# Encoder block in fp32 on one core: another order of the opening, unread matmuls in TensorE's waits, and tiles on 512-byte addresses

## The chip, the core and the metric

The kernel runs on one core of a Trainium2 chip. The metric is device time in microseconds. Before the change three executions took 1934.24, 1934.75 and 1935.72 us, median 1934.75.

## The reference, cut to what matters

One layer with 256 tokens and width 2048, all in float32:

```
mod = silu(c) @ w_ada + b_ada            # c is one vector of 2048; mod is 9 vectors of 2048
sh1,sc1,gt1, sh2,sc2,gt2, sh3,sc3,gt3 = split(mod, 9)
n   = rms_norm(x, g_ffn1) * (1 + sc1) + sh1
h   = x + 0.5*gt1 * ((silu(n @ w1_gate) * (n @ w1_up)) @ w1_down)     # 2048 -> 5632 -> 2048
n   = rms_norm(h, g_mix) * (1 + sc2) + sh2
q,k,v = split(n @ w_qkv);  o = attention(q, k, v)                     # 16 heads of 128
h   = h + gt2 * (o @ w_o)
n   = rms_norm(h, g_ffn2) * (1 + sc3) + sh3
out = h + 0.5*gt3 * ((silu(n @ w2_gate) * (n @ w2_up)) @ w2_down)
```

## The kernel before

**Layout.** The activations lie transposed, features on the 128 partitions and the 256 tokens along them: `h` is 16 tiles (k = 0 to 15) of 128x256, loaded as four DMAs of 512 KB (`h<-in_x_dram`, L515). Each weight is streamed once as 656 tiles of 128x1024 (`rw`, 512 KB, one DMA of SyncE's queue each, L77), four of them in flight. To keep float32's precision, each weight tile is split: ScalarE writes the rounded part (`hiw`, L84), VectorE the rest (`low`, L91), and a product is three matmuls in the fp32r format (`mm3`, L222 to 225): high by high, high by low, low by high. The activations are split in the same way: `nx[k]` holds both parts of tile k of the normed input, side by side, `hd` of the hidden layer, `ox` of the attention's output.

**Order.** The order on each engine is that in which the code issues; no scheduler moves anything. A class `Flow` counts units, one weight tile each: `step()` (L114) splits the tiles ahead of their use and runs what was due; `before1` (L552) does this by hand for the first units. The work goes: opening; first half-FFN up (`up_start`, L405, for the first K1 = 3 tiles k and two column groups of 1024, into all eight PSUM banks `pa`; then `up_pass`, banks `pu`), down (`ffn_down`, L433, banks `pd`); norm; q, k, v and attention (`pqv`, `pqk`, `pqq`, then `psc`, `po`); output projection (`pso`); norm; second half-FFN.

**Modulation.** `mod` is made on VectorE: for a vector j and a tile k, two instructions of 128x1024 (`ada_use`, L196) multiply a tile of `w_ada` with silu(c), which lies spread over all partitions in `cb`, and sum it into one column of `acc`. The 288 tiles of `w_ada` (512 KB each) go through SyncE's queue too.

**The opening** (L501 to L567): DMAs of c, spread over the partitions by the DMA (2 x 512 KB), of the vectors `vec` (112 KB), of the modulation tiles (1, 0) and (0, 0) (scale and shift of tile 0; 4 x 512 KB), then x, then weights and the modulation tiles of k = 1 and 2. ScalarE and VectorE make silu(c) on `cb`; VectorE sums the four modulation tiles of k = 0; ScalarE squares x (L538), and 16 float32 matmuls with a matrix of ones (L540) sum the squares into `pstat`. Then follow the factor of the norm `rs` (`rstd_act`, L245 and 246, on ScalarE, `rstd_dve`, L250 to 253, on VectorE), tile 0's norm (`p0` L305 on VectorE, `p1` L308 on ScalarE, `p2` L311 on VectorE) and the first two weight tiles' split. For k = 1 and 2 VectorE first sums four modulation tiles, then norms, then splits.

**The two later norms.** `Stat.finish` (L290) sums the squares by two float32 matmuls: L292 for those of all tiles but the last, L293 for the last, which VectorE has just squared (L272). Then the same factor and norm follow, and TensorE has no other work until the first `nx` is there.

Of the kernel before, what the change touches and what calls it, by code (L numbers as in the profile page):

```python
# [15 lines left out]
P = 128  # L16
S = 256
# [133 lines left out]
def build(tc, a):  # L151
    nc = tc.nc
    with ExitStack() as ctx:
# [15 lines left out]
        epst = cp.tile([P, 1], F32, name="epst")  # L169
        nc.vector.memset(epst, EPS)  # L170
# [3 lines left out]
        G1, GO, BA = 0, 48, 80  # L174
# [10 lines left out]
        gat = cp.tile([P, 2, KT], F32, name="gat")  # L185

        def ada_use(j, k, b, raw):
# [6 lines left out]
            if b == 1:  # L194
                init = acc[:, j, 0, k : k + 1]
            nc.vector.tensor_tensor_reduce(  # L196
                out=raw, in0=raw, in1=cb[:, b * CW : (b + 1) * CW], scale=scale, scalar=init,
                op0=ALU.mult, op1=ALU.add, accum_out=acc[:, j, b, k : k + 1])
# [5 lines left out]
        def mod(j, k):  # L204
            assert (j, k) in modded, (j, k)
            return acc[:, j, 1, k : k + 1]
# [33 lines left out]
        def rstd_tiles(w, tag):  # L240
            ts = [sp.tile([P, S], F32, tag="nt", bufs=4, name="rt")[:, :w] for i in range(2)]
            return ts + [sp.tile([P, w], F32, tag=tag, bufs=2, name=tag)]

        def rstd_act(ps, n, ts):
            nc.scalar.activation(ts[0], ps, AF.Ln, scale=1.0 / n, bias=epst)  # L245
# [15 lines left out]
        class Stat:  # L261
# [28 lines left out]
            def finish(self):  # L290
                self.ps = bank("pstat")[:, :S]
                nc.tensor.matmul(self.ps, ones, self.acc, start=True, stop=False)  # L292
                nc.tensor.matmul(self.ps, ones, self.last, start=False, stop=True)  # L293

# [138 lines left out]
        def ffn_down(jg, stat=None, out=None):  # L433
# [54 lines left out]
            if stat is not None:  # L488
                stat.add(stat.square(h[d], True))
                stat.finish()  # L490
# [10 lines left out]
        nc.sync.dma_start(cb[:, :CW], a["c"][0].partition_broadcast(P))  # L501
        nc.sync.dma_start(vec, a["vecs"])
        nc.sync.dma_start(cb[:, CW:], a["c"][1].partition_broadcast(P))
        early = {}

        def early_load(k):
            for j in (1, 0):
                t = big("ra")
                for b in range(2):
                    early[k, j, b] = t[:, 4 * b : 4 * b + 4, :].rearrange("p a s -> p (a s)")  # L510
                    nc.sync.dma_start(early[k, j, b], a["w_ada"][j * KT + k, b])

        early_load(0)
        for q in range(4):
            nc.sync.dma_start(h4[q], a["x"][q])  # L515
        fl.fetch(1)
        for k in range(1, K1):
            early_load(k)
            fl.fetch(min(2 * k + 1, RAWW - 1))
        thc = big("thc")  # L520
        for b in range(2):
            th = thc[:, 4 * b : 4 * b + 4, :].rearrange("p a s -> p (a s)")
            cs = slice(b * CW, (b + 1) * CW)
            nc.scalar.activation(th, cb[:, cs], AF.Tanh, scale=0.5)
            nc.vector.scalar_tensor_tensor(cb[:, cs], th, 1.0, cb[:, cs], ALU.add, ALU.mult)
        ln_exp_set()
        bias3 = vec[:, BA : BA + 9 * KT].rearrange("p (n j k) -> p n j k", n=3, j=3)
# [6 lines left out]
        for q in range(4):  # L534
# [4 lines left out]
            for i in range(4):  # L539
                nc.tensor.matmul(ps1, ones, sq[:, i, :], start=q + i == 0, stop=q + i == 6)  # L540
        rt = rstd_tiles(S, "rs")

        def early_use(k):
            for j in (1, 0):
                for b in range(2):
                    ada_use(j, k, b, early[k, j, b])
# [5 lines left out]
        def before1(k, j):  # L552
            if j == 0:
                early_use(k)
                if k == 0:
                    rstd_act(ps1, D, rt)
                    rstd_dve(ps1, D, rt)
                norm_now(k, rt[2], 1, 0)
# [4 lines left out]
            fl.to_hi(fl.u)  # L563
            fl.to_lo(fl.u)
            fl.u += 1
            return fl.hi.pop(fl.u - 1), fl.lo.pop(fl.u - 1)
# [408 lines left out]
```

## Time and profile before

| | us |
|---|---|
| median of three runs | 1934.75 |
| the profiled execution, its own time | 1935.05 |
| its span, from the first to the last instruction | 1933.2 |
| TensorE busy | 1890.7 (98%) |
| VectorE busy | 1527.3 (79%) |
| ScalarE busy | 895.7 (46%) |
| first matmul | 15.35 |
| first matmul of `up_start` | 29.92 |

Names before and behind the arrow are the tiles written and read; a count stands behind an x. PE is TensorE, DVE VectorE, ACT ScalarE, SP SyncE, SPq its sequencer. Matmuls overlap: how often TensorE takes one is read from the distance between two starts, not from an instruction's own duration. In the table by windows, PEclk is the clock granted to TensorE as a share of full speed.

### The profile page before, as it was taken

What the parts mean: (1) busy time and instruction counts of PE and PEld (TensorE: products, weight loads), DVE (VectorE), ACT (ScalarE), POOL (GpSimd) and SP (SyncE); (2) the same over time, 40 slices, a digit from 0 to 9 for tenths busy, and PEclk for the clock granted to TensorE, in tenths of its full rate; (3) what the DMA queues carried; (4) which work ended last, traced back from release to release, by engine and by line L of the source; (5) the groups of instructions that cost most, each with busy time, mean ns of one, the idle gap of its engine ahead of it and who ended that gap; (6) DMA issues with size and microseconds to landing.
All of it is one profiled execution on the core that took longest, in us unless ns stands there. A gap on an engine that the chain in (4) does not pass through costs nothing.

```text
span 1933.2 us, 24958 instructions
## 1 busy us (share of the span) xinstructions
PE 1890.7 (98%) x9024; PEld 1582.3 (82%) x9024; DVE 1527.3 (79%) x2082; ACT 895.7 (46%) x1223; POOL 0.7 (0%) x6
## 2 busy tenths in 40 slices
PE   5999999999999999999999998999999999999999
PEld 4788888888888888788888997888888888888887
DVE  5889988888898889678887988777787888876444
ACT  3664444444444444455555544654443544443432
POOL 0000000000000000000000000000000000000000
PEclk8999999999999999999999999999999999999999
DMA  8899987777799999576766656998888777787664
GB/s 308 325 350 308 311 294 251 248 247 258 244 348 353 350 368 343 196 241 215 249 202 214 206 182 198 307 308 277 273 270 268 222 211 226 215 289 250 201 195 126
DMA packets 141101, 504.89 MB, mean 261 GB/s; under 512 B 15665, under 2 KB 17969, under 8 KB 140977
## 3 DMA queue, kind: packets, MB, share of 16 engines
q1 hardware_dynamic: 140976, 503.30, 77.9%
q8 instruction: 70, 1.15, 0.2%
q14 instruction: 55, 0.44, 0.1%
HBM read 501.14 MB, written 2.10 MB: 260 GB/s over the span
## 4 chain that ended last, share of the span: by engine, by line
PE 93%; DVE 5%; DMA 1%; ACT 0%; issue 0%; SPq 0%; DVEq 0%; ACTq 0%
PE pu L223 16%; PE pu L225 16%; PE pu L224 16%; PE pd L225 6%; PE pd L223 6%; PE pd L224 6%; PE pd L228 4%; PE pd L229 2%; PE pqv L223 2%; DVE low L91 2%; PE pqv L225 2%; PE pqv L224 2%; PE pqk L223 2%; PE pqk L224 2%; PE pqk L225 2%; PE pqq L223 2%
## 5 line engine op out<-in xcount | busy, mean ns | idle before, releaser
L84 ACT CAST hiw<-rw 128x1024 fp32r<-128x1024 f32 x656 | 692.0, 1056 | 960.8 <-PE pu L225 449.6
L91 DVE TENSOR_TENSOR low<-rw,hiw 128x1024 fp32r<-128x1024 f32 x656 | 802.2, 1224 | 346.3 <-issue 132.1
L223 PE MATMUL pu<-hiw,nx 128*128 128x512 f32 x1352 | 527.9, 390 | 0.4 <-ACT pt L348 0.4
L225 PE MATMUL pu<-hiw,nx 128*128 128x512 f32 x1352 | 526.3, 389 | 0.0
L224 PE MATMUL pu<-low,nx 128*128 128x512 f32 x1352 | 526.1, 389 | 0.0
L223 PEld LDWEIGHTS pu<-hiw,nx 128*128 128x128 f32 x1352 | 253.8, 188 | 52.9 <-ACT pt L348 0.8
L225 PEld LDWEIGHTS pu<-hiw,nx 128*128 128x128 f32 x1352 | 253.7, 188 | 52.9
L224 PEld LDWEIGHTS pu<-low,nx 128*128 128x128 f32 x1352 | 253.8, 188 | 52.2
L223 PE MATMUL pd<-hiw,hd 128*128 128x512 f32 x528 | 207.5, 393 | 0.0
L225 PE MATMUL pd<-hiw,hd 128*128 128x512 f32 x528 | 207.3, 393 | 0.0
L224 PE MATMUL pd<-low,hd 128*128 128x512 f32 x528 | 205.6, 389 | 0.0
L196 DVE CUSTOM_DVE_ANT_0 ra<-ra,cb,acc 128x1024 f32<-128x1024 f32 x144 | 187.2, 1300 | 0.2
L228 PE MATMUL pd<-hd,hiw 128*128 128x512 f32 x352 | 124.7, 398 | 0.0
L224 PEld LDWEIGHTS pd<-low,hd 128*128 128x128 f32 x528 | 99.1, 188 | 22.2
L225 PEld LDWEIGHTS pd<-hiw,hd 128*128 128x128 f32 x528 | 99.2, 188 | 22.1
L223 PEld LDWEIGHTS pd<-hiw,hd 128*128 128x128 f32 x528 | 99.2, 188 | 20.4
L352 DVE TENSOR_TENSOR pt<-pt,pu 128x512 f32<-128x512 f32 x176 | 112.5, 680 | 0.0
L229 PE MATMUL pd<-hd,low 128*128 128x256 f32 x352 | 98.9, 281 | 0.0
L196 DVE CUSTOM_DVE_ANT_0 ra<-ra,cb,vec 128x1024 f32<-128x1024 f32 x64 | 81.9, 1279 | 0.0
L228 PEld LDWEIGHTS pd<-hd,hiw 128*128 128x128 f32 x352 | 66.2, 188 | 16.2
L223 PE MATMUL pso<-ox,hiw 128*128 128x256 f32 x256 | 73.1, 285 | 0.0
L225 PE MATMUL pso<-ox,low 128*128 128x256 f32 x256 | 72.4, 283 | 0.0
(139 smaller groups left out, 1972.6 us busy)
## 6 DMA issues: line engine op xcount, KB each, us to landing
ra<-in_w_ada_dram SPq DMA_DIRECT2D x288, 512.0 KB, 5.0
rw<-in_w_d_dram SPq DMA_DIRECT2D x176, 512.0 KB, 4.6
rw<-in_w_c_dram SPq DMA_DIRECT2D x154, 512.0 KB, 4.3
rw<-in_w_b_dram SPq DMA_DIRECT2D x121, 512.0 KB, 4.8
rw<-in_w_qkv_dram SPq DMA_DIRECT2D x96, 512.0 KB, 3.8
rw<-in_w_a_dram SPq DMA_DIRECT2D x63, 512.0 KB, 4.9
rw<-in_w_o_dram SPq DMA_DIRECT2D x32, 512.0 KB, 3.8
rw<-in_w_s_dram SPq DMA_DIRECT2D x14, 512.0 KB, 4.3
```

Of the source, the lines that this page charges most:

```text
L84: self.nc.scalar.copy(t, self.raw[self.nhi])
L91: self.nc.vector.tensor_tensor(t, self.raw.pop(self.nlo), self.hi[self.nlo].bitcast(F32), ALU.subtract)
L196: nc.vector.tensor_tensor_reduce(out=raw, in0=raw, in1=cb[:, b * CW : (b + 1) * CW], scale=scale, scalar=init, op0=ALU.mult, op1=ALU.add, ...
L223: nc.tensor.matmul(out, lh, rh, start=first, stop=False, **kw)
L224: nc.tensor.matmul(out, lh, rl, start=False, stop=False, **kw)
L225: nc.tensor.matmul(out, ll, rh, start=False, stop=last, **kw)
L228: nc.tensor.matmul(ps, lh, r.rearrange("p t s -> p (t s)"), start=first, stop=False)
L229: nc.tensor.matmul(ps[:, :S], ll, r[:, 0, :], start=False, stop=last)
L352: nc.vector.tensor_tensor(part[G][:, j, t, :], part[G][:, j, t, :], ps[t], ALU.add)
```

## The change

**DMA order.** x is loaded right behind `vec`, then the scale's modulation tiles of k = 0, then `w_zero` (2 x 512 KB: the columns of `w_ada` that make the shift of tile 0, with the contraction on the partitions), then the first weight tiles. c is no longer loaded spread. On SyncE's queue the opening was (`cb` is c, `ra` a modulation tile, `h` is x, `rw` a weight tile):

```order
L501 DMA cb<-in_c_dram 128x1024
L502 DMA vec<-in_vecs_dram 128x224
L503 DMA cb<-in_c_dram 128x1024
L511 DMA ra<-in_w_ada_dram 128x1024 x4
L515 DMA h_80<-in_x_dram 128x1024
L515 DMA h_81<-in_x_dram 128x1024
L515 DMA h_82<-in_x_dram 128x1024
L515 DMA h_83<-in_x_dram 128x1024
L77 DMA rw<-in_w_s_dram 128x1024 x2
```

and in the changed kernel it is:

```order
L515 DMA vec<-in_vecs_dram 128x224
L517 DMA h_78<-in_x_dram 128x1024
L517 DMA h_79<-in_x_dram 128x1024
L517 DMA h_80<-in_x_dram 128x1024
L517 DMA h_81<-in_x_dram 128x1024
L521 DMA ra<-in_w_ada_dram 128x1024 x2
L523 DMA wz<-in_w_zero_dram 128x1024 x2
L77 DMA rw<-in_w_s_dram 128x1024 x2
```

Six DMAs of 512 KB no longer stand ahead of x.

**c on 16 columns.** silu(c) is made on a 128x16 tile (`sc2`, printed `sc`). VectorE multiplies the identity with its columns (`dg`, four of 128x512), four float32 matmuls with the ones spread them over the partitions into PSUM (`pc`), and ScalarE copies them into `cb` between the squares of x.

**Squares and shift.** VectorE adds the squares in pairs, so that 8 float32 matmuls of 256 columns are left of 16. The shift of tile 0 comes of 16 float32 matmuls of one column each (`pm`) and one small VectorE instruction (`shift0`).

**Unread matmuls.** Fp32r matmuls of 512 columns go into a bank `idle` that nobody reads: 7 at the start, 4 behind each quarter of the squares, and at the two later norms 4 between the two sums and 13 behind them. TensorE's order in the opening was (`pstat` the sums of squares, `pa` the first product):

```order
L540 MATMUL pstat<-sq_151,ones 128x256 x8
L540 MATMUL pstat<-sq_162,ones 128x256 x8
L223 MATMUL pa_176<-hiw,nx_85 128x512
L224 MATMUL pa_176<-low,nx_85 128x512
L225 MATMUL pa_176<-hiw,nx_85 128x512
```

and is:

```order
L536 MATMUL idle<-nx_97 128x512 x7
L551 MATMUL pc<-dg,ones 128x512 x4
L569 MATMUL pstat<-sq_172,ones 128x256 x2
L536 MATMUL idle<-nx_97 128x512 x4
L569 MATMUL pstat<-sq_172,ones 128x256 x2
L536 MATMUL idle<-nx_97 128x512 x4
L569 MATMUL pstat<-sq_191,ones 128x256 x2
L536 MATMUL idle<-nx_97 128x512 x4
L569 MATMUL pstat<-sq_191,ones 128x256 x2
L536 MATMUL idle<-nx_97 128x512 x4
L574 MATMUL pm<-sc_140,wz 128x1 x16
L224 MATMUL pa_238<-hiw,nx_82 128x512
```

The sums of squares are half as many, and the unread matmuls, the spreading and the one-column matmuls stand in one line ahead of the first product.

**Tile 0's norm and split.** In `before1` the high part of a weight tile is made ahead of the norm, its low part between the norm's second and third step, and the fetch of later tiles moves along. On VectorE, from the norm's factor on (`rt`, `rs`) to the modulation of k = 1, stood:

```order
L253 SCALAR_TENSOR_TENSOR rs<-rt,rs 128x256
L305 SCALAR_TENSOR_TENSOR nt<-h_80,acc,rs 128x256
L311 SCALAR_TENSOR_TENSOR nx_85<-nt,acc,nx_85 128x256
L91 TENSOR_TENSOR low<-rw,hiw 128x1024 x2
L196 ISA ra,acc<-ra,cb,gin,gsc 128x1024
```

and now stands:

```order
L254 SCALAR_TENSOR_TENSOR rs<-rt,rs 128x256
L315 SCALAR_TENSOR_TENSOR nt<-h_78,acc,rs 128x256
L582 TENSOR_SCALAR acc<-pm,vec 128x1
L91 TENSOR_TENSOR low<-rw,hiw 128x1024
L321 SCALAR_TENSOR_TENSOR nx_82<-nt,acc,nx_82 128x256
L91 TENSOR_TENSOR low<-rw,hiw 128x1024
L197 ISA ra,acc<-ra,cb,gin,gsc 128x1024
```

The instruction that waits for the one-column matmuls now stands ahead of the low parts and of the whole modulation of k = 1.

**Addresses.** `acc` is half as large, `epst` is padded to 32 columns, and the small tiles `rq`, `ss`, `mx`, `sm` move into one pool. With that each tile of 512 bytes or more per partition behind `vec` starts at a multiple of 512 bytes. Before, counted modulo 512, `nx`, `rw`, `hiw`, `low` and `ra` started at 160, `hd` at 352, `ox` and the attention's tiles at 416 (`vh`, `vl` at 352), `h` and `cb` at 32.

The diff, cut to its core:

```diff
-        acc = cp.tile([P, 9, 2, KT], F32, name="acc")
+        nc.gpsimd.memset(nx[KT - 1].bitcast(F32), 0.0)
+        acc = cp.tile([P, 9, KT], F32, name="acc")
+        epst = cp.tile([P, 32], F32, name="epst")
...
-            def finish(self):
+            def finish(self, busy=None):
+                def keep_busy(n):
+                    if busy is not None:
+                        idle = bank("idle")
+                        for i in range(n):
+                            nc.tensor.matmul(
+                                idle, busy[:, 0, :P], busy.rearrange("p t s -> p (t s)"), start=True, stop=True)
                 self.ps = bank("pstat")[:, :S]
                 nc.tensor.matmul(self.ps, ones, self.acc, start=True, stop=False)
+                keep_busy(4)
                 nc.tensor.matmul(self.ps, ones, self.last, start=False, stop=True)
+                keep_busy(13)
...
+        keep_busy(7)
+        nc.scalar.activation(sc2, cc, AF.Tanh, scale=0.5)
         ln_exp_set()
+        nc.vector.scalar_tensor_tensor(sc2, sc2, 1.0, cc, ALU.add, ALU.mult)
+        for q in range(4):
+            dg = eighths("dg")[0][:, :512].rearrange("p (a b) -> p a b", a=4)
+            nc.vector.tensor_tensor(
+                dg, ident.unsqueeze(1).broadcast_to([P, 4, P]),
+                sc2[:, 4 * q : 4 * q + 4].unsqueeze(2).broadcast_to([P, 4, P]), ALU.mult)
+            nc.tensor.matmul(pcs[q], ones, dg.rearrange("p a b -> p (a b)"), start=True, stop=True)
...
             nc.scalar.activation(sq, h4[q], AF.Square)
-            for i in range(4):
-                nc.tensor.matmul(ps1, ones, sq[:, i, :], start=q + i == 0, stop=q + i == 6)
+            nc.scalar.copy(cb[:, q * 512 : (q + 1) * 512], pcs[q])
+            if q == 3:
+                ada_use(1, 0, 0, early[0, 1][0])
+            nc.vector.tensor_tensor(sq[:, 0:2, :], sq[:, 0:2, :], sq[:, 2:4, :], ALU.add)
+            for i in range(2):
+                nc.tensor.matmul(ps1, ones, sq[:, i, :], start=q + i == 0, stop=q + i == 4)
+            keep_busy(4)
+        ada_use(1, 0, 1, early[0, 1][1])
+        for c in range(KT):
+            nc.tensor.matmul(
+                pm[:, 0:1], zero[c // 8][:, c % 8 * P : (c % 8 + 1) * P], sc2[:, c : c + 1],
+                start=c == 0, stop=c == KT - 1)
...
         def before1(k, j):
+            u = fl.u
             if j == 0:
-                early_use(k)
+                if k:
+                    for i in (1, 0):
+                        for b in range(2):
+                            ada_use(i, k, b, early[k, i][b])
+                fl.to_hi(u)
+                p0, p1, p2 = norm_parts(k, rt[2], 1, 0)
+                p0()
                 if k == 0:
-                    rstd_act(ps1, D, rt)
-                    rstd_dve(ps1, D, rt)
-                norm_now(k, rt[2], 1, 0)
+                    shift0()
+                p1()
+                fl.to_hi(u + 1)
+                fl.to_lo(u)
+                p2()
+                fl.to_lo(u + 1)
```

More of the change, by code (lines that the diff above doesn't have):

```diff
@@ L499, in big, with eighths @@
             return hp.tile([P, 8, S], F32, tag="hid", name=nm)
[L501 removed]
+        def eighths(nm):
+            t = big(nm)
+            return [t[:, 4 * b : 4 * b + 4, :].rearrange("p a s -> p (a s)") for b in range(2)]
         nc.sync.dma_start(vec, a["vecs"])
[L503 to L511, printed above, removed]
@@ L519, in build, with keep_busy @@
             fl.fetch(min(2 * k + 1, RAWW - 1))
[L520 to L525, printed above, removed]
-        ln_exp_set()
+        idle = bank("idle")
+        def keep_busy(n):
+            for i in range(n):
+                nc.tensor.matmul(
+                    idle, nx[KT - 1][:, 0, :P], nx[KT - 1].rearrange("p t s -> p (t s)"), start=True, stop=True)
```

60 lines of the change are left out of this document (36 added, 24 removed).

## The prediction, made before the changed kernel was run

> **What bounds the kernel now.** I read the page first: the shares of the engines, and who makes up the chain that ended last.
>
> ```profile
> PE 1890.7 (98%) x9024; PEld 1582.3 (82%) x9024; DVE 1527.3 (79%) x2082; ACT 895.7 (46%) x1223; POOL 0.7 (0%) x6
> PE 93%; DVE 5%; DMA 1%; ACT 0%; issue 0%; SPq 0%; DVEq 0%; ACTq 0%
> ```
>
> TensorE works 98% of the span and is 93% of the chain. So time can be won in three ways only: TensorE waits less, runs at a higher clock, or takes its matmuls closer together. Next, the view of TensorE's waits:
>
> ```profile
> PE pstat L540 <- ACT sq L538: 15.4, 1, 15.4
> PE pa L223 <- ACT hiw L84: 6.3, 3, 4.4
> PE pqv L223 <- ACT nx L308: 3.4, 1, 3.4
> PE pa L223 <- ACT nx L308: 3.4, 1, 3.4
> ```
>
> The first two stand in the opening, the last two at the two later norms. The timeline of the opening shows what they wait for (start, duration, engine, line; in brackets the idle time and what ended it):
>
> ```profile
> 14.24 1.06 ACT L538 ACTIVATE sq<-h 128x1024 f32<-128x1024 f32 x1 [4.15 <-DMA h<-in_x_dram]
> 15.35 10.19 PE L540 MATMUL pstat<-sq,ones 128*128 128x256 f32 x32 [15.35 <-ACT sq L538]
> 15.53 1.06 ACT L538 ACTIVATE sq<-h 128x1024 f32<-128x1024 f32 x1 [0.22 <-DMA h<-in_x_dram]
> 18.09 1.06 ACT L538 ACTIVATE sq<-h 128x1024 f32<-128x1024 f32 x1 [0.23 <-DMA h<-in_x_dram]
> 25.58 0.47 ACT L245 ACTIVATE rt<-pstat,epst 128x256 f32<-128x256 f32 x1 [6.43 <-PE pstat L540]
> 27.91 0.48 DVE L305 SCALAR_TENSOR_TENSOR nt<-h,acc,rs 128x256 f32<-128x256 f32 x1
> 28.43 0.51 ACT L308 ACTIVATE nx<-nt,acc 128x256 fp32r<-128x256 f32 x1 [1.93 <-DVE nt L305]
> 29.92 0.79 PE L223 MATMUL pa<-hiw,nx 128*128 128x512 f32 x1 [4.38 <-ACT hiw L84]
> 31.18 0.80 PE L224 MATMUL pa<-low,nx 128*128 128x512 f32 x1 [0.46 <-DVE low L91]
> 32.18 1.34 DVE L196 CUSTOM_DVE_ANT_0 ra<-ra,cb,gin 128x1024 f32<-128x1024 f32 x1
> 39.39 0.49 PE L223 MATMUL pa<-hiw,nx 128*128 128x512 f32 x1 [0.83 <-ACT hiw L84]
> 41.64 1.34 DVE L196 CUSTOM_DVE_ANT_0 ra<-ra,cb,gin 128x1024 f32<-128x1024 f32 x1
> 48.84 0.50 PE L223 MATMUL pa<-hiw,nx 128*128 128x512 f32 x1 [1.05 <-ACT hiw L84]
> 56.07 0.50 PE L223 MATMUL pu<-hiw,nx 128*128 128x512 f32 x1 [0.41 <-ACT pt L348]
> ```
>
> The first quarter of x is there at 14.24, the sums take TensorE until 25.54, the first product comes at 29.92. From then on VectorE sets the pace, 9.46 us for each k (32.18 to 41.64), until TensorE runs through from 56.07. The stretches by granted clock (PEclk behind the engines):
>
> ```profile
> 28.30:35.10 6.80, 4.71 (x10) 3.43 (x11) 5.74 (x9) 2.39 (x3) 0.00 (x0) 0.50 0.89 317
> 782.60:789.50 6.90, 6.09 (x14) 4.79 (x15) 5.29 (x10) 3.42 (x6) 0.00 (x0) 0.51 0.18 55
> 1188.80:1195.70 6.90, 5.59 (x13) 4.43 (x14) 3.58 (x7) 2.02 (x4) 0.00 (x0) 0.51 0.24 76
> ```
>
> Behind each of the two later norms TensorE works 6.9 us at half clock. What one matmul of 512 columns costs is the distance of starts, at half clock (11 rows, the first and the last) and at full clock (98 rows):
>
> ```profile
> 784.43 0.63 PE L225 MATMUL pqv<-hiw,nx 128*128 128x512 f32 x1
> 788.70 0.63 PE L223 MATMUL pqk<-hiw,nx 128*128 128x512 f32 x1
> ...
> 239.80 0.39 PE L223 MATMUL pu<-hiw,nx 128*128 128x512 f32 x1
> 261.78 0.39 PE L224 MATMUL pu<-low,nx 128*128 128x512 f32 x1
> ```
>
> That is 4.27 / 10 = 0.427 and 21.98 / 97 = 0.2266. Note that 0.2266 is more than half of 0.427: 0.2135 would be half.
>
> **The change part by part.** The sum is made against the profiled execution's own 1935.05 us; the median of the runs is 0.3 lower.
>
> *x earlier.* Squares start 1.28 us apart ((18.09 - 14.24) / 3), as the DMAs land. Six DMAs of this size no longer stand ahead of x: 7.7 us. The first square can start at 6.5, the fourth at 10.4. The weights behind x land earlier too; the modulation tiles of k = 1, places 7 to 10 behind x's last, are there by 10.4 + 10 x 1.28 = 23.2. All of it holds only if the queue starts up as fast without c's spread loads.
>
> *TensorE's line in the opening.* It becomes longer, and sets the end. Unread matmuls start once GpSimd has zeroed their operand, about 2: 7 x 0.427 = 3.0, to 5. A float32 matmul of 256 columns is two instructions, each 10.19 / 32 = 0.318 on the mean of a stretch in which the clock rose from half to full, so between 0.21 and 0.43. The spreading has 8 instructions of double width: 3.4 at full, 6.8 at half clock. If the clock rises some 6 us after the first matmul, as between 15.35 and the end of that stretch, they end near 10. The sums: 16 instructions at 0.21, and three times 4 unread at 0.227 between them: 3.4 + 2.7, to 16. ScalarE and VectorE are done before: four squares of 1.06 and three copies of half a square's size from 6.5 on end near 12.4, and one modulation instruction (1.34) and a pair sum (half of a 128x1024 instruction, 0.6) give the last addend near 14. Behind it 4 unread (0.9), to 17. Then the one-column matmuls, 32 instructions of which the weights' load is all the work. The trace has none; near it are the matmuls of 256 columns (127 rows, first and last), 0.12 each with their load, and the load's own duration:
>
> ```profile
> 1144.83 0.28 PE L225 MATMUL pso<-ox,low 128*128 128x256 f32 x1
> 1159.95 0.28 PE L225 MATMUL pso<-ox,low 128*128 128x256 f32 x1
> ...
> L223 PEld LDWEIGHTS pu<-hiw,nx 128*128 128x128 f32 x1352 | 253.8, 188 | 52.9 <-ACT pt L348 0.8
> L91 DVE TENSOR_TENSOR low<-rw,hiw 128x1024 fp32r<-128x1024 f32 x656 | 802.2, 1224 | 346.3 <-issue 132.1 <-PE pd L224 69.0 <-PE pu L224 65.6
> ```
>
> 32 x 0.12 to 32 x 0.188 is 3.8 to 6.0; I take 4.9, between them: the loads can overlap, but float32 may not let them. So `shift0` runs at 16 + 0.9 + 4.9 = 21.8; its ends are 19 (full clock from 5 on, loads at 0.12) and 25 (half clock until the spreading is done, loads at 0.188). The norm's factor is no limit: 16 + 2.33 (25.58 to 27.91) = 18.3.
>
> *Behind shift0.* VectorE's queue holds the low part (1.22), `p2` (as L305, 0.48), the second low part (1.22), and the modulation of k = 1, all behind the wait for the one-column matmuls. That modulation starts at 21.8 + 3.1 = 24.9 instead of 32.18: 7.3 won. Its own tiles have landed. Per k the low part no longer waits for ScalarE: from the norm's start to the next modulation were 4.27 us (27.91 to 32.18), now 0.48 + 1.22 + 0.48 + 1.22 = 3.4: 0.9 won at k = 1. At k = 2 the second product waits for the low part, before 3.27 behind the norm's start (27.91 to 31.18), now 0.48 + 1.22 and a little: 1.4 won. Together 9.6. TensorE idles 2 to 3 us before k = 1 and k = 2; one more stretch at half clock there would cost up to 1.6. I take 8.5, ends 5 and 12. That is what TensorE's steady run from 56.07 starts earlier; nothing behind it gives time back, since VectorE and the DMAs are not in TensorE's waits there.
>
> *Unread matmuls at the later norms.* The gaps:
>
> ```profile
> 779.26 0.70 PE L293 MATMUL pstat<-sq,ones 128*128 128x256 f32 x2 [1.12 <-DVE sq L272]
> 783.41 0.80 PE L223 MATMUL pqv<-hiw,nx 128*128 128x512 f32 x1 [3.45 <-ACT nx L308]
> 1185.96 0.70 PE L293 MATMUL pstat<-sq,ones 128*128 128x256 f32 x2 [0.61 <-DVE sq L272]
> 1190.11 0.80 PE L223 MATMUL pa<-hiw,nx 128*128 128x512 f32 x1 [3.45 <-ACT nx L308]
> ```
>
> 13 x 0.227 = 2.95 behind 779.96 ends at 782.9, before 783.41; behind 1186.66 at 1189.6, before 1190.11. So they cost nothing and have 0.5 us to spare; should they run at half clock they would end 2 us late, each time. If the gap no longer counts as idle, 14 and 13 matmuls take 0.2266 each: 6.09 - 3.17 = 2.9 and 5.59 - 2.95 = 2.6. Of these 5.5 I take 5.3, as the second k's norm then just keeps up; ends 0 and 5.5.
>
> *Addresses.* This touches every matmul, and is the term that I know least of. That places may matter is in the trace. With a weight tile (160 modulo 512) as the moving operand, 512 columns cost 0.2266 where `nx` (160 too) is the stationary one, and more where `hd` (352) is. And the pair of 512 and 256 columns with `hd` moving and the weights (160) stationary costs more than its like (98 and 121 rows, first and last):
>
> ```profile
> 619.79 0.39 PE L224 MATMUL pd<-low,hd 128*128 128x512 f32 x1
> 641.99 0.39 PE L225 MATMUL pd<-hiw,hd 128*128 128x512 f32 x1
> ...
> 733.73 0.40 PE L228 MATMUL pd<-hd,hiw 128*128 128x512 f32 x1
> 754.93 0.40 PE L228 MATMUL pd<-hd,hiw 128*128 128x512 f32 x1
> ```
>
> 22.20 / 97 = 0.2289 against 0.2266, and 21.20 / 120 = 0.1767 against (0.2266 + 0.12) / 2 = 0.1733. If it is the difference of the places that costs, as all places become equal, 1584 matmuls win 2.3 ns and 704 win 3.4: 6 us. If it is something else about `hd`, nothing. I take 3.
>
> [...]
>
> Sum: 1935.05 - 8.5 - 5.3 - 3 = 1918.25; against the median, **1918**. Its own range, from the ends named, is 1911 to 1930.
>
> **The rivals.**
>
> *The matmuls come closer together.* At half clock a matmul takes exactly its 512 columns, at full clock 13 ns more than half of that. So at full clock something else than the array, perhaps the reading of operands that start off a boundary, sets the rhythm, and starts at 512 bytes could take it away. For it: 0.2266 against 0.2135, and the differing places. Against it: the same excess would stand there if each matmul simply costs 13 ns to begin. Of the 9024 matmuls all but 352 transposes and 48 of float32, by the code, are fp32r: 8624. Half of the excess gone is 8624 x 6.7 ns = 57 us: 1861; all of it 115: 1803. Chance 0.22. [...]
>
> *The matmuls come further apart.* Equal places mean that weights' load and moving operand read at the same place of each 512 bytes; if that collides, the pitch rises instead. The rows with `hd` moving show the size: 0.1767 x 2 - 0.12 = 0.2334, 7 ns above 0.2266. On some 7300 matmuls of 512 columns (8624 without the 1312 of 256) that is 50 us: 1971 with the forecast's other terms and no 3. It decides from 17 us / 8624 = 2 ns per matmul on. Against it: `nx` and `hiw`, equal before, are the cheapest rows. Chance 0.09.
>
> *The opening gives nothing, or the clock falls all the same.* At half clock throughout TensorE's line is 2 + 3 + 6.8 + 6.8 + 6.8 + 6.0 = 31 long, `shift0` comes behind where the norm's factor was, and unread matmuls end 2 us late at each later norm: 1930 to 1939. For it: the clock fell in the opening and behind each norm. Against it: it rose again within 7 us each time. If only the clock's part fails while the opening wins, it is 1924, within the forecast's own range. Chance of the first 0.08, 0.04 of it within 0.2%.
>
> **How the numbers follow.** Forecast 0.61; closer 0.22; further apart 0.09; nothing won 0.08. A measurement of this kernel tells about 0.2% (4 us) from no change. Faster by more: 0.61 + 0.22 + 0.03 = 0.86; within: 0.04; slower: 0.09 + 0.01 = 0.10. The range of 8 in 10 takes the forecast's own (0.61) and reaches down to 1850, which takes in the half excess and what lies between (0.16), and up to 1930, which takes in part of the weaker openings (0.03).
>
> **What would show it.** In the changed profile: the first square near 6.5, the first product near 22.4, the first `pu` near 47.5; PEclk 1.00 in the 7 us behind each later norm; no wait of `pqv` or `pa` longer than 1 us there. The distance of two `pu` starts decides on the rivals: 0.2266 is the forecast, 0.220 or 0.2135 the closer one, above 0.229 the slower one. I am wrong if the first product comes after 27, if half clock stands behind the norms, or if that distance moves by over 1%.

## The result, and the profile after

| kernel | runs | median us | range us | ratio to before, 95% interval |
|---|---|---|---|---|
| before | 4 | 1935.03 | 1934.24 to 1935.72 | |
| changed | 4 | 1913.88 | 1912.90 to 1915.07 | 0.9889 (0.9875 to 0.9902) |

The profiled execution of the changed kernel took 1914.67 us (span 1912.9), that of before 1935.05 (1933.2): 20.4 us less. The page after, its row of engines:

```profile
PE 1896.2 (99%) x9105; PEld 1591.3 (83%) x9105; DVE 1526.6 (80%) x2086; ACT 895.5 (47%) x1226; POOL 1.2 (0%) x7
```

TensorE is still the bound; it has 81 more instructions and 5.5 us more of busy time, in a span 20 us shorter. Where the 20 us come from is read best from the same instruction in both traces. The timeline of before, TensorE, the first or last instruction of each part:

```profile
530.56 0.39 PE L223 MATMUL pd<-hiw,hd 128*128 128x512 f32 x1
777.54 0.59 PE L292 MATMUL pstat<-sqa,ones 128*128 128x256 f32 x2
791.79 0.39 PE L223 MATMUL pqv<-hiw,nx 128*128 128x512 f32 x1
1135.50 0.39 PE L224 MATMUL po<-pl,vh 128*128 128x256 f32 x1 [2.77 <-DVE pl L235]
1184.65 0.70 PE L292 MATMUL pstat<-sqa,ones 128*128 128x256 f32 x2 [1.38 <-DVE sqa L286]
1203.71 0.39 PE L223 MATMUL pa<-hiw,nx 128*128 128x512 f32 x1
1682.19 0.39 PE L223 MATMUL pd<-hiw,hd 128*128 128x512 f32 x1
1929.05 0.28 PE L229 MATMUL pd<-hd,low 128*128 128x256 f32 x1
```

The same instructions in the changed kernel, with the first `pu` (before: 56.07) ahead:

```profile
45.14 0.39 PE L224 MATMUL pu<-hiw,nx 128*128 128x512 f32 x1
519.37 0.39 PE L224 MATMUL pd<-hiw,hd 128*128 128x512 f32 x1
763.51 0.59 PE L300 MATMUL pstat<-sqa,ones 128*128 128x256 f32 x2
775.11 0.39 PE L224 MATMUL pqv<-hiw,nx 128*128 128x512 f32 x1
1119.29 0.39 PE L225 MATMUL po<-pl,vh 128*128 128x256 f32 x1 [2.73 <-DVE pl L236]
1169.94 0.70 PE L300 MATMUL pstat<-sqa,ones 128*128 128x256 f32 x2 [1.37 <-DVE sqa L287]
1186.53 0.39 PE L224 MATMUL pa<-hiw,nx 128*128 128x512 f32 x1
1664.84 0.39 PE L224 MATMUL pd<-hiw,hd 128*128 128x512 f32 x1
1908.86 0.28 PE L230 MATMUL pd<-hd,low 128*128 128x256 f32 x1
```

Each difference of starts is the gain so far; the step from one to the next is what the part between them gave:

| part | gain so far at its end | of this part |
|---|---|---|
| opening, to the first `pu` | 56.07 - 45.14 = 10.93 | 10.93 |
| first up passes | 530.56 - 519.37 = 11.19 | 0.26 |
| first second product (`pd`) | 777.54 - 763.51 = 14.03 | 2.84 |
| first later norm | 791.79 - 775.11 = 16.68 | 2.65 |
| q, k, v and attention, to the last head | 1135.50 - 1119.29 = 16.21 | -0.47 |
| from there to the last norm's sums | 1184.65 - 1169.94 = 14.71 | -1.50 |
| second later norm | 1203.71 - 1186.53 = 17.18 | 2.47 |
| second up passes | 1682.19 - 1664.84 = 17.35 | 0.17 |
| second `pd` | 1929.05 - 1908.86 = 20.19 | 2.84 |

So: opening 10.9, places 5.7, norms 5.1, and a loss of 2.0 in the attention that the prediction did not have. The timeline of the changed opening:

```profile
4.64 1.06 ACT L563 ACTIVATE sq<-h 128x1024 f32<-128x1024 f32 x1 [0.35 <-DMA h<-in_x_dram]
4.97 4.74 PE L551 MATMUL pc<-dg,ones 128*128 128x512 f32 x8
14.91 1.02 PE L569 MATMUL pstat<-sq,ones 128*128 128x256 f32 x4
16.70 3.63 PE L574 MATMUL pm<-sc,wz 128*128 128x1 f32 x32
20.37 0.22 DVE L582 TENSOR_SCALAR acc<-pm,vec 128x1 f32<-128x1 f32 x1 [1.57 <-PE pm L574]
21.18 0.79 PE L224 MATMUL pa<-hiw,nx 128*128 128x512 f32 x1 [0.85 <-ACT nx L318]
23.24 1.33 DVE L197 CUSTOM_DVE_ANT_0 ra<-ra,cb,gin 128x1024 f32<-128x1024 f32 x1
31.57 1.34 DVE L197 CUSTOM_DVE_ANT_0 ra<-ra,cb,gin 128x1024 f32<-128x1024 f32 x1
37.83 0.68 PE L224 MATMUL pa<-hiw,nx 128*128 128x512 f32 x1 [2.07 <-ACT nx L318]
```

x's first square is at 4.64 (before 14.24), the first product at 21.18 (29.92), the modulation of k = 1 at 23.24 (32.18), that of k = 2 8.33 us later (9.46). The first later norm, and four stretches by granted clock (PEclk is the first number behind the busy times of the five engines): the 7 us behind each later norm's gap, then the stretch behind the last head's wait, and the wait itself:

```profile
765.58 3.34 PE L296 MATMUL idle<-hd 128*128 128x512 f32 x13
769.38 0.50 PE L224 MATMUL pqv<-hiw,nx 128*128 128x512 f32 x1 [0.47 <-ACT nx L318]
...
769.40:776.40 7.00, 7.00 (x30) 5.45 (x31) 6.42 (x12) 4.45 (x7) 0.00 (x0) 1.00 0.26 92
1175.50:1182.50 7.00, 7.00 (x31) 5.67 (x32) 6.35 (x9) 3.63 (x5) 0.00 (x0) 1.00 0.47 155
1119.90:1123.50 3.60, 3.60 (x20) 3.60 (x19) 1.68 (x4) 0.75 (x2) 0.00 (x0) 0.53 0.48 167
1116.60:1120.00 3.40, 0.71 (x6) 0.71 (x7) 3.37 (x7) 0.81 (x1) 0.00 (x0) 1.00 0.85 282
```

The first norm's gap is 0.47 us instead of 3.45, and behind both norms the clock stays at full. But behind the last head there is a new piece of half clock, 3.4 us long, though the wait of 2.7 us before it stood in the kernel before as well. And the decider of the prediction, the distance of two `pu` starts (98 rows, first and last), is (260.70 - 238.72) / 97 = 0.2266 us, as before:

```profile
238.72 0.39 PE L226 MATMUL pu<-hiw,nx 128*128 128x512 f32 x1
...
260.70 0.39 PE L224 MATMUL pu<-hiw,nx 128*128 128x512 f32 x1
```

### The profile page after: what moved, and what is told of

Same layout as the page of the kernel before. It is cut to its first block, busy times and chain, and to the rows that moved or that the text cites. A ratio compares the mean times of both kernels' runs of the same rounds, so it can differ in the third digit from the quotient of the medians.

```text
span 1912.9 us, 25124 instructions
## 1 busy us (share of the span) xinstructions
PE 1896.2 (99%) x9105; PEld 1591.3 (83%) x9105; DVE 1526.6 (80%) x2086; ACT 895.5 (47%) x1226; POOL 1.2 (0%) x7
## 4 chain that ended last, share of the span: by engine, by line
PE 94%; DVE 4%; issue 1%; ACT 0%; POOL 0%; POOLq 0%; DVEq 0%
PE pu L224 16%; PE pu L226 16%; PE pu L225 16%; PE pd L225 6%; PE pd L226 6%; PE pd L224 6%; PE pd L229 4%; PE pd L230 2%; PE pqv L224 2%; PE pqk L224 2%; PE pqq L224 2%; PE pqk L225 2%; PE pqk L226 2%; PE pqq L225 2%; PE pqv L226 2%; PE pqq L226 2%
## 5 line engine op out<-in xcount | busy, mean ns | idle before, releaser
L224 PEld LDWEIGHTS pd<-hiw,hd 128*128 128x128 f32 x528 | 99.1, 188 | 20.4
L224 PE MATMUL pso<-ox,hiw 128*128 128x256 f32 x256 | 73.9, 289 | 0.0
L225 PE MATMUL pso<-ox,hiw 128*128 128x256 f32 x256 | 73.1, 286 | 0.0
```

The costliest lines, as they stand in the source:

```text
L224: nc.tensor.matmul(out, lh, rh, start=first, stop=False, **kw)
L225: nc.tensor.matmul(out, lh, rl, start=False, stop=False, **kw)
```

## The experiments

Twelve kernels. The theory: the three parts of the change act by themselves (opening by TensorE's line, norms by the clock, second products by equal places). The rivals stand with each run. Medians in us; the changed kernel has 1913.9, 0.9889.

| run | median | ratio to before, 95% interval |
|---|---|---|
| e1 all places at 160 | 1911.83 | 0.9884 (0.9870 to 0.9897) |
| e2 hidden tiles at 192 | 1920.86 | 0.9926 (0.9913 to 0.9938) |
| e9 hidden tiles at 256, then 64 | 1919.27 | 0.9923 (0.9911 to 0.9936) |
| e10 before, all places equal | 1929.04 | 0.9971 (0.9961 to 0.9982) |
| e3 norms without unread matmuls | 1916.68 | 0.9910 (0.9897 to 0.9924) |
| e4 sums without unread matmuls | 1911.82 | 0.9881 (0.9866 to 0.9896) |
| e12 start without unread matmuls | 1914.78 | 0.9899 (0.9885 to 0.9912) |
| e5 shift on VectorE | 1912.40 | 0.9886 (0.9873 to 0.9900) |
| e6 x behind | 1918.99 | 0.9922 (0.9909 to 0.9934) |
| e7 two more waits filled | 1911.81 | 0.9885 (0.9870 to 0.9900) |
| e8 three edits | 1909.55 | 0.9872 (0.9858 to 0.9885) |
| e11 three edits, another last head | 1908.50 | 0.9868 (0.9853 to 0.9883) |

### Places

e1 puts an unread tile of 160 bytes ahead of c's, e2 one of 192 ahead of the hidden tiles alone, e9 one of 256 in the first feed-forward and of 64 in the second:

```
+        pad = cp.tile([P, 40], F32, name="pad")                       # e1
+        hp.tile([P, 48], F32, tag="pad", bufs=1, name="pad")          # e2; e9: 64 columns
+        hp2.tile([P, 48], F32, tag="pad2", bufs=1, name="pad2")       # e2; e9: 16 columns
```

e10 is the kernel before; `gsc` and `gat` move ahead of `nx`, `epst` behind it with 16 columns, and the small tiles `ss`, `mx`, `sm`, `rq` into the pool `cp`.

> The changed kernel with one unread tile of 160 bytes ahead of c's tile, so that every tile behind it begins at 160 modulo 512, all at the same place, and none at a boundary of 512 bytes. Theory (it is the equal place of weights' tiles and activations that made the second products cheaper, not the boundary): the distance of two pd starts stays at 0.2266 us with the weights moving and the pair of 512 and 256 columns at 0.347; time 1913.9 us, ratio to the kernel before 0.989, as the changed kernel. Rival (the boundary itself): 0.2289 and 0.353 come back and with them 5.8 us: 1919.7, 0.992.

> The changed kernel with an unread tile of 192 bytes ahead of the hidden tiles of both feed-forwards, so that hd lies at 192 modulo 512 while weights and nx stay at 0: the same distance between them as in the kernel before (352 - 160). Theory (unequal places cost): pd with the weights moving goes back from 0.2266 to 0.2289, the pair from 0.347 to 0.353, 2.9 us for each of the two second products: 1919.7 us, ratio 0.992; the attention part as in the changed kernel. Rival (something else in the layout, such as places that are multiples of 32 and not of 64): 192 is a multiple of 64, so nothing comes back: 1913.9, 0.989.

> The changed kernel with the hidden tiles of the first feed-forward at 256 modulo 512 and those of the second at 64, weights and nx at 0. It asks which distances cost. Theory (a distance of 256 is harmless, as in the kernel before the attention's last product had it, 416 against 160, at 0.120 us per 256 columns, and what counts is the distance modulo 128, in which 192 is 64): the first second product stays at 0.2266 and 0.347 us, the other goes to 0.2289 and 0.353 and costs 2.9 us: 1916.8 us, ratio 0.9905. Rival 1 (every unequal place costs alike): both go back, 5.8 us, 1919.7, 0.992. Rival 2 (only places that are no multiples of 128, or only large distances, matter in another way): neither costs, 1913.9, 0.989.

> The kernel before with its tiles regrouped alone, so that weights, nx, hidden tiles and the attention's tiles all lie at 448 modulo 512: nothing of the opening and no unread matmul is taken over. Theory (the places give their 5.8 us by themselves, whatever stands around them): 1934.4 - 5.8 = 1928.6 us, ratio 0.997, up to 1.5 us more if a half-clock piece appears behind the last head's wait. Rival (part of it shows only with the other edits, or the multiple of 512 is needed after all): less than half of it, 1931.5 or more, 0.9985.

What each place costs is the time from the first `pd` to the next part (first feed-forward) or to the last matmul (second). For e2 and then e9, from their timelines:

```profile
519.25 0.39 PE L224 MATMUL pd<-hiw,hd 128*128 128x512 f32 x1
766.25 0.59 PE L300 MATMUL pstat<-sqa,ones 128*128 128x256 f32 x2
1668.84 0.39 PE L224 MATMUL pd<-hiw,hd 128*128 128x512 f32 x1
1915.72 0.28 PE L230 MATMUL pd<-hd,low 128*128 128x256 f32 x1
```

```profile
517.55 0.39 PE L224 MATMUL pd<-hiw,hd 128*128 128x512 f32 x1
761.68 0.59 PE L300 MATMUL pstat<-sqa,ones 128*128 128x256 f32 x2
1663.04 0.40 PE L224 MATMUL pd<-hiw,hd 128*128 128x512 f32 x1
1913.36 0.28 PE L230 MATMUL pd<-hd,low 128*128 128x256 f32 x1
```

| hidden tiles less weights, modulo 512 | kernel | first `pd` part | second |
|---|---|---|---|
| 192 (352 less 160) | before | 246.98 | 246.86 |
| 192 (192 less 0) | e2 | 247.00 | 246.88 |
| 0 (both 0) | changed | 244.14 | 244.02 |
| 0 (both 160) | e1 | 244.15 | 244.04 |
| 0 (both 448) | e10 | 244.13 | 244.01 |
| 256, then 64 | e9 | 244.13 | 250.32 |

For these products it is the distance, not the boundary: 160 and 448 do as well as 0, and 192 costs 2.85 us in each product whether the tiles stand at 352 or at 192, a multiple of 64. The expectation for e1 and e2 holds there, the rivals fall. e1's median is nevertheless 2.1 us below the changed kernel's: its trace has no half clock behind the last head's wait, which is worth 1.5 us. So a difference of 2 us between two medians need not come from the edit. In e10 each product gains the same 2.85 us with nothing of the opening or of the norms taken over. That its last matmul is 5.79 us earlier than in before, and its median 5.4 us lower, so near to 5.7, is partly luck: behind the last head its trace has a new piece of half clock that costs 1.5 us, and at the two norms half clock falls more into the idle gaps and costs 0.5 and 1.0 us less. Of e9's theory one half holds (256 costs nothing), the other falls: 64 costs 6.3 us, more than twice as much as 192, so it is not the distance modulo 128. That e9's median lies near rival 1's 1919.7 is chance; its trace shows another split. Why 64 is worse than 192 stays open.

### The norms

e3 leaves the unread matmuls out at the two later norms:

```
-                stat.finish(hid[0])
+                stat.finish()
-                        hst.finish(ox[0])
+                        hst.finish()
```

> The changed kernel without the unread matmuls at the two later norms. Theory: the gaps of 3.45 us stand there again and behind each of them half clock, 3.4 to 6.9 us of it, which costs up to 2.65 us at the first and 2.48 at the second, as the two traces differ there: 1919.0 us, ratio 0.9915 (from 0.990 if the gaps fall so that the clock drops for one piece of 3.4 us alone). Rival (the clock does not follow the gaps): no change, 1913.9, 0.989.

The stretch behind the first norm (that behind the second, 1175 to 1182, has 0.51 too):

```profile
768.80:775.80 7.00, 6.12 (x15) 4.83 (x16) 5.39 (x10) 3.46 (x6) 0.00 (x0) 0.51 0.17 49
```

Half clock is back, 6.8 us each. Against the changed kernel the starts fall back by 2.64 us at the first norm and 2.22 at the second, 4.9 of the 5.1 expected. The profiled execution is only 3.6 us longer (1918.28 against 1914.67), since 1.5 us come back behind the last head: in this execution no half clock follows its wait. The median rises by 2.8; the executions scatter from 1916.19 to 1918.28.

### The opening

e4 takes the four unread matmuls from behind each quarter of the sums, e12 the seven at the start, e5 replaces the one-column matmuls, e6 moves x's loads:

```
-            keep_busy(4)                                               # e4
-        keep_busy(7)                                                   # e12
-        pm = bank("pm") ... matmul(pm[:, 0:1], ...)                    # e5
+        for b in range(2): ada_use(0, 0, b, zero[b])                   # e5: zero holds w_ada[0]
-        for q in range(4): dma_start(h4[q], a["x"][q])                 # e6: the same two lines
+        for q in range(4): dma_start(h4[q], a["x"][q])                 # behind w_zero's loads
```

One thing bears on all four. The opening's code is the same in the changed kernel, e1, e2, e3 and e9, and yet in their traces the first `pu` starts at 45.14, 44.80, 44.87, 45.46 and 43.28: the pieces in which the clock is granted (last section) fall at other places (full clock from 7.27 us in the changed kernel, from 4.67 in e1, from 5.05 in e2). A difference of up to 2.2 us in the first `pu` between two traces is therefore not by itself an effect of the edit.

> The changed kernel without the four unread matmuls behind each quarter of x's sums in the opening (16 of 0.227 us, 3.6 us of TensorE's line); the seven at the start stay. Theory 1 (TensorE's line sets the end of the opening, as the prediction has it, and the clock does not need them): the last quarter's sum then waits only for its operand, which is there at 13.1, and starts at 13.1 instead of 14.91; the one-column matmuls start near 13.8 instead of 16.70, the tile's shift comes at 17.5 instead of 20.37, and the time falls by 2.9 us to 1911.0, ratio 0.9874. Theory 2 (they keep the clock up): half clock in the sums and the one-column matmuls, the shift comes no earlier, 1913.9 or up to 2 us more, 0.989 to 0.990.

Timeline and stretches of e4 (sums of the last quarter, one-column matmuls, shift; then PEclk during and behind):

```profile
12.98 1.13 PE L569 MATMUL pstat<-sq,ones 128*128 128x256 f32 x4 [1.30 <-DVE sq L567]
13.95 4.80 PE L573 MATMUL pm<-sc,wz 128*128 128x1 f32 x32
18.79 0.22 DVE L581 TENSOR_SCALAR acc<-pm,vec 128x1 f32<-128x1 f32 x1 [1.82 <-PE pm L573]
...
16.20:22.90 6.70, 5.85 (x20) 4.89 (x20) 4.84 (x7) 2.13 (x3) 0.00 (x0) 0.50 1.02 419
```

Both theories are half right. The one-column matmuls start 2.75 us earlier, as theory 1 has it, but from 16.2 on the clock is halved and they take 4.80 us instead of 3.63; the shift is 1.58 earlier, not 2.9. The sums themselves ran at full clock (PEclk 1.00 from 13.0 to 16.1), so it was not they that needed the unread matmuls. The shift at 18.79 is earlier than in those five traces (19.65 to 20.57). The first `pu`, 1.44 us earlier, lies within their scatter, and the medians differ by 2.1 us, with intervals that overlap.

> The changed kernel without the seven unread matmuls at the very start; those behind the sums stay. Theory (they let the clock rise one piece of 3.41 us earlier, which c's spreading needs, since TensorE's line sets the end of the opening): the clock rises at about 10.7 instead of 7.3 us, the spreading ends near 11.2 instead of 9.5, and the opening with it: 1915.6 us, from 1914 to 1916.2, ratio 0.990. Rival (the spreading's own matmuls raise the clock as soon, or the sums wait for x anyway): 1913.9, 0.989.

By the traces' clock records the clock rose at 7.13 us after the span's start in e12, in the changed kernel at 7.27 (there the distance of two spreading matmuls goes from 0.85 to 0.43 us): the spreading's own matmuls, from 4.13 on, raised it as soon, where the seven unread ones had held them back to 4.97. The first `pu` is at 44.86 instead of 45.14. The median is 0.9 us higher, within what this measurement can tell: in these two executions the seven gave nothing that can be seen. It may be otherwise where the pieces fall earlier: with the seven the clock rose at 4.67 us in e1 and at 5.05 in e2, less than 1 us behind 4.13, where the spreading starts in e12. Even there the first product, at 20.46 and 20.48, is only 0.3 us earlier than e12's 20.77.

> The changed kernel with the shift of tile 0 made by VectorE again: its two half rows are loaded where the tiles of the one-column matmuls were, and two modulation instructions (1.34 us each) stand behind those of the scale; the 32 one-column matmuls are gone. Theory 1 (they saved VectorE work that lay in the path): the shift comes later than 20.37 us by what the two instructions take less the 1.57 us that VectorE waited, +1.1 us, 1915.0, ratio 0.9895. Theory 2 (VectorE stood idle from 14.36 to 16.48 while TensorE summed, so it can do them for 0.6 us of delay, and TensorE's 3.6 us of one-column matmuls were the later of the two): the normalised tile 0 is there 1.2 us earlier, 1912.7, ratio 0.9883.

The activation of tile 0 in e5, on ScalarE:

```profile
18.22 0.51 ACT L318 ACTIVATE nx<-nt,acc 128x256 fp32r<-128x256 f32 x1 [1.25 <-DVE nt L315]
```

It is at 18.22 instead of 20.62, 2.4 us earlier, of which 0.86 is a clock that rose earlier during the spreading (its last sums at 14.05 instead of 14.91). The first `pu` is at 43.04, 2.1 us earlier. In the five traces with the changed kernel's opening this activation starts at 19.90 to 20.82, so theory 2 holds in direction, and its size with what the clock adds: in this opening the one-column matmuls were the later of two ways, since VectorE had a hole while TensorE summed. How much of it reaches the total isn't shown: 43.04 is only just ahead of the five (43.28 to 45.46), and the medians differ by 1.5 us, within the intervals.

> The changed kernel with x's four loads put back behind the two loads of the scale's rows and the two of the one-column matmuls' tiles. The squares come 5.1 us later (four loads of 1.28). Theory 1 (TensorE's line, not x, sets the end of the opening): only the last quarter's sum is held back, from 14.91 to 17.1, and the time rises by 2.2 us: 1916.1, ratio 0.990. Theory 2 (x's arrival sets the end): all 5.1 us come back: 1919.0, ratio 0.9915.

The first and the last quarter's sums of e6, and PEclk in the first 3.3 us of them:

```profile
12.01 2.08 PE L569 MATMUL pstat<-sq,ones 128*128 128x256 f32 x4 [3.37 <-DVE sq L567]
19.06 1.02 PE L569 MATMUL pstat<-sq,ones 128*128 128x256 f32 x4
...
12.00:15.30 3.30, 3.29 (x8) 2.66 (x9) 1.87 (x3) 3.30 (x5) 0.00 (x0) 0.50 1.02 420
```

Neither expectation has it right. The first sums are 2.46 us later (12.01 instead of 9.55), but TensorE had waited 3.37 us for them, the clock fell, and the first quarter with its unread matmuls took 3.47 us instead of 1.79; the last sums come 4.15 us later. The first `pu` is at 49.55, 4.41 later, the median 5.1 higher. x's place in the queue was thus worth nearly as much as theory 2 said, by way of TensorE's line and its clock. It is the one part of the opening whose price these four runs show clear of the scatter. The pair sums, c on 16 columns and the new order of tile 0's norm and split were not taken out by any run, so how the rest of the opening's 10.9 us divides among them stays open.

### The last head, and a better version

e7 fills two more waits, ahead of the third k and ahead of the last head's product with v; e8 and e11 take e4's edit and the first of these, and change the last head's order:

```
+    if k == 2 and G + j == 0: 8 x matmul(pa[0][0][0], zeros, zeros, start=False)   # e7, e8, e11
+    if hd == NH - 1: 11 x matmul(pob, ox[0], ox[0])                                # e7
-PLAN_L = (..., (9, 11, 14, 15))
+PLAN_L = (..., (9, 11, 13, 15))                                                    # e8
-    (c0 + 1, c_hi, 0), (c0 + 1, c_lo, 1)
+    (c0, c_hi, 2), (c0, c_lo, 2)                                                   # e11, last head only
```

> The changed kernel with unread matmuls in two more of TensorE's waits: eight (1.8 us) ahead of the third k of the opening, where it waits 2.07 us, with an operand of zeros added into a bank in use; eleven (2.5 us) ahead of the last head's product with v, where it waits 2.73 us. Theory (a wait of 2 us or more within one of the 3.41 us pieces by which the clock is granted costs the next piece half its speed): half clock behind the third k goes, 1.6 us; that behind the last head goes, 1.5 us in those executions that have it: 1911.0 us, from 1910.8 to 1912.3, ratio 0.9875. Rival (the clock falls there for another reason, or unread matmuls delay what follows): 1913.9 or more, 0.989.

```profile
34.94 1.98 PE L424 MATMUL pa<-nx 128*128 128x512 f32 x8
37.13 0.49 PE L224 MATMUL pa<-hiw,nx 128*128 128x512 f32 x1 [0.21 <-ACT nx L318]
...
1114.00:1122.00 8.00, 7.79 (x52) 6.96 (x51) 6.48 (x11) 2.81 (x5) 0.00 (x0) 1.00 0.60 201
```

The eight fill the third k's wait, the eleven the last head's. From the third k's first product to the first `pu` it is 6.10 us (37.13 to 43.23) instead of 7.31, 1.2 us less and not 1.6, since the products there now wait a little for VectorE's low parts. e9 shows the same without unread matmuls: it has the wait (2.06 us), but no half clock falls behind it, and it takes 6.11 us (37.17 to 43.28). Behind the last head the clock stays at 1.00. The profiled execution is 3.4 us shorter than the changed kernel's (1911.23 against 1914.67): 1.2 at the third k, 1.5 behind the last head, and 0.7 that the edit doesn't explain, since the first product is already 0.7 us earlier (20.47). The medians differ by 2.1, expected 2.9. The theory holds; the difference of the medians alone would not have shown it.

> The changed kernel with three edits that are meant to add up: no unread matmuls behind the sums of the opening (measured alone: 1911.8), eight unread ones ahead of the third k (1.6 us), and the last head's transposes one step of the plan earlier, so that its low part is not asked for in the step that makes it: the wait of 2.73 us goes, and with it the chance of half clock behind it (1.5 us). Theory: 2.1 + 1.6 + 2.7 to 4.2 us below the changed kernel: 1907 us, from 1905.5 to 1908, ratio 0.9855. Rival (the earlier transposes wait for the softmax's division instead, and the wait only moves): 1910.2, 0.987.

> The changed kernel with three edits: no unread matmuls behind the sums of the opening (alone 1911.8), eight unread ones ahead of the third k (1.6 us by the two traces), and the last head's high and low part queued right behind its transposes instead of one step later, so that VectorE's low part of it no longer stands behind a weight's low part, an attention sum and a modulation instruction. Theory (the wait of 2.73 us before the last product with v is that queue): the wait goes, and with it half clock behind it in the executions that had it: 1911.8 - 1.6 - 2.7 - about 0.7 = 1906.8 us, from 1906 to 1908, ratio 0.986. Rival (VectorE now waits for the transposes and the weights' low parts behind come late, as when the transposes were put a step earlier and 2.3 us of wait came there): 1909.5 or more, 0.987.

The longest wait of the attention in the view of waits, e8 and then e11:

```profile
PE pP L821 <- DVE sc L815: 2.3, 1, 2.3
```

```profile
PE pso L225 <- DVE ox L846: 1.6, 1, 1.6
```

In both the wait before the last product with v is gone and another stands near it: in e8, as its rival said, the transposes wait 2.3 us for the softmax's division, in e11 the first output product that needs the last head waits 1.6 for its low part. No half clock follows either: the output products of 256 columns behind it start 0.12 us apart. So it seems to be VectorE's work for the last head that sets this place, and an earlier place in its queue for one step only brings the next to light. Against the changed kernel's trace e8 wins 2.0 us from the first output product to the last norm's sums and e11 2.4, of which the missing half clock makes 1.5. Both medians are some 2 us above their theory (2.5 and 1.7). e11 has the lowest median, 1908.50 us, 5.4 us below the changed kernel, but its interval overlaps that of e8, so the two aren't told apart.

## Why the prediction was right

The time, 1918 predicted and 1913.9 measured, is 4 us lower than forecast and within the forecast's own range; no rival came. That it is no further off is partly luck: against the trace the gain of the opening was put 2.4 us too low and that of the addresses 2.7, and a loss of 2.0 that the sum didn't have took part of that back. By its steps:

- **x earlier, TensorE's line in the opening.** The order of events was right, each a little early: first square 4.64 (said 6.5), spreading to 9.7 (10), sums to 15.9 (16), one-column matmuls 3.63 us long (4.9, ends 3.8 to 6.0; below the lower end, 0.113 each; the loads of their weights filled 3.77), shift at 20.37 (21.8), first product 21.18 (22.4). That TensorE's line sets the end, with the clock as part of it, e4 and e5 bear out: with a shorter line tile 0's shift and activation come earlier. e6 shows that x's arrival still counts, by way of this line.
- **Behind shift0.** 8.9 us won at the modulation of k = 1 (said 7.3), 1.1 by the next k (0.9), 0.9 more until the first `pu` (1.4): 10.9 where 8.5 was taken and 12 the upper end. The mis-sized term is the first, by 1.6 us, of which 1.4 is the early shift. The size is partly a matter of the execution: the same opening wins 12.8 in e9. The half-clock stretch taken off as a risk did come, at the third k (before had one at the second, from 41.96), and cost 1.2 us of the 1.6 named: from that k's first product to the first `pu` it is 7.31 us (37.83 to 45.14), and 6.10 in e7, without it.
- **Unread matmuls at the later norms.** 2.65 and 2.47 against 2.9 and 2.6; 0.47 us were to spare, said 0.5. Right, and e3 undoes it.
- **Addresses.** 3 us were taken between 0 and 6; it was 5.7, nearly the whole of what the two rows offered. The mechanism, the difference of the places, is confirmed by e1, e2 and e10; the half taken off for doubt was the error. e9 adds that not each difference costs: 256 apart it is 244.13 us, as with none, and 64 apart 250.32.
- **The sum's gap.** It had no term for the attention, and there 2.0 us were lost: 1.5 by the new half clock behind the last head, 0.47 spread over the attention. That stretch, from behind the norm to the last head, took 343.71 us in before, 344.18 in the changed kernel, 344.13 to 344.16 in the seven other runs with the attention's tiles at 0 that have this wait, but 343.70 in e1 (all at 160) and 343.81 in e10 (448). So the places seem to have a hand in it, here against the multiple of 512; by which matmuls stays open. So 10.9 + 5.7 + 5.1 - 2.0 and 0.4 in the up passes make the 20.2 of the trace, against 16.8 said.
- **Rivals.** "Closer together" and "further apart" fall by their decider, 0.2266. The 13 ns above half of the half-clock distance stay at every place tried (0, 160 and 448 all show 244.0 to 244.2 us of `pd`), so they are not a matter of boundaries. "Opening gives nothing" falls at 21.18 for the first product.

## What to carry to other kernels

Follow the same instruction through both traces and take differences of starts: the gain by stage shows terms that cancel in the total, here a loss of 2 us that nobody had costed. Look at the places of the two operands' tiles modulo 512 bytes: in the second products here 0 and 256 apart cost nothing, 192 apart 2.85 us and 64 apart 6.3 us in 244, while the boundary itself (0, 160 or 448 for both) made no difference. Look behind TensorE's waits for a second price: here half clock followed those of 2.07 us (third k) and 2.73 us (last head) and cost 1.2 and 1.5 us, and filling them with unread matmuls in e7 saved that price but not the wait. It did not follow the wait of 2.06 us in e9 and that of 2.77 in before, so judge it by the trace and over several executions. And before a difference between two traces is put down to an edit, look at how much the same stretch differs between traces in which its code is the same; here it was 2.2 us for the opening.

## What the runs showed of the hardware

The traces show the clock granted in pieces. In the clock records of the changed kernel's trace the pieces of half clock begin 20.918, 37.985 and 1120.01 us from the span's start and last 3.413 us each; their starts lie 17.07 and 1099.09 us apart, 5 and 322 times 3.4133. Whether a piece was at half clock went with how busy TensorE was in the one before. In the fourteen traces each piece at full clock in which TensorE was busy for 47% of the time or less was followed by half clock. Of those from 48 to 57% some were and some were not. Of the busier ones only pieces with one-column matmuls in them were (below). In before, for instance, half clock followed the pieces from 24.89, 38.54, 779.24 and 1185.42 us (busy 19, 53, 21 and 21%), and none followed that from 1182.01 (57%). The last head's wait is the same in both kernels (2.77 and 2.73 us), but in before it fell across two pieces:

```profile
1130.80:1134.20 3.40, 1.93 (x17) 1.72 (x15) 3.37 (x8) 1.04 (x1) 0.00 (x0) 1.00 0.81 284
1134.20:1137.60 3.40, 2.10 (x17) 2.10 (x18) 3.37 (x7) 0.75 (x2) 0.00 (x0) 1.00 0.45 157
```

TensorE was busy 57% and 62% of them, and the clock stayed; in the changed kernel one piece took the whole wait (busy 0.71 of 3.40 us, shown with the result) and the next had half clock. So 2.7 us of idling within one piece were enough here.

One-column matmuls did not keep the clock up: in all eleven kernels that have them the clock fell behind a piece filled with them in part or whole, though TensorE was busy for 75 to 100% of that piece. In the changed kernel it fell from 20.92, though TensorE was busy with them for 2.83 us of the 3.4 before:

```profile
17.50:20.90 3.40, 2.83 (x26) 2.75 (x25) 1.76 (x5) 0.61 (x2) 0.00 (x0) 1.00 1.02 418
```

At half clock the time of a matmul went with its columns: 512 took 0.427 us, and the 256 of an output product in the changed kernel (13 rows, first and last) (1123.15 - 1120.59) / 12 = 0.2133, half of it.

```profile
1120.59 0.41 PE L224 MATMUL pso<-ox,hiw 128*128 128x256 f32 x1
...
1123.15 0.41 PE L224 MATMUL pso<-ox,hiw 128*128 128x256 f32 x1
```
